# Squares summed on VectorE at seven stage fronts, twelve more low parts by accumulating DMA, and half of the second panel ahead of the first mean, in a two-block transformer kernel

## The chip, the core and the metric

The kernel runs on one core of one Trainium2 chip. The metric is the device time of one launch in microseconds (us). The engines are named as the profile names them: PE (TensorE, matrix products), PEld (its weight loads), DVE (VectorE), ACT (ScalarE), POOL (GpSimd) and SP (SyncE, which issues the DMAs of raw weights). Each engine works through its own instructions in the order in which they were written into its queue; an instruction whose operands are not there holds up all that is queued behind it on that engine.

## What is computed

Two blocks over a sequence of 512 rows with model width 1024, all in fp32. Cut to what matters:

```python
# first block, layer 0 (causal conformer convolution) and layer 1 (forgetting attention)
hn = rmsnorm(h, mix_norm[i])
h = h + conformer_conv(hn, ...)          # layer 0: hn @ w_pw1, a * sigmoid(g), 31 taps, layernorm, silu, @ w_pw2
h = h + fox_attention(hn, ...)           # layer 1: 16 heads, softmax with cumulated forget gates, @ w_o
hn = rmsnorm(h, ffn_norm[i])
h = h + square(relu(hn @ ffn_w1[i])) @ ffn_w2[i]
h = h + sigmoid(rmsnorm(h, ple_norm[i]) @ ple_w_gate[i]) * (p[i] @ ple_w_proj[i])
...
x = rmsnorm(h, final_norm)               # end of the first block
# second block
h = rms_norm(x, mix_norm_gain)           # -> w_in: recurrent, block-sparse and memory branches, gates, w_out
x = x + merged @ w_out
h = rms_norm(x, ffn_norm_gain)
x = x + (gelu(dwconv(h @ w_gate)) * (h @ w_up)) @ w_down
return rms_norm(x, final_norm_gain)
```

The rows matter here for one thing: every stage begins with a root mean square over the 1024 columns of h, which needs the squares of all eight column groups of h summed and averaged before the stage's results can be scaled.

## The kernel before, in words

**Layout.** The 512 rows lie along the free dimension, the 1024 columns in eight tiles of 128 partitions (f = 0 to 7), so h is eight tiles of 128x512. Products run on PE at fp32 accuracy as three products of reduced-precision halves: `mm3` issues hi times xh, hi times xl, lo times xh, where a weight is hi + lo and an activation xh + xl.

**Weights.** They come as panels of 128x2048 fp32 (1 MB), in the order of `_KEYS`, through SP's queue into two raw buffers (`load`). `splitting` cuts a panel in four pieces of 128x512; `part` casts a piece to hi on ACT and subtracts to get lo, on DVE, or on POOL for the families in `LO_POOL` (`pw1`, `vm`, `o`). For the panels in `SEVEN`, `lows_by_dma` makes three of the four lo pieces another way: ACT writes minus raw into lo, rounded as hi is, and a DMA on POOL's queue adds the raw weight from memory to it, which leaves raw minus hi with no work for DVE (`accumulate`). hi and lo have two buffers each, so a panel's piece can be written when PE has read that of the panel two before it. `prefetch` loads and starts to split the next panel while the current one is used; the delay `PREFETCH` holds the splitting back.

**Fronts.** `Front` takes the h tiles of a new stage as they are finished: `split_into` makes xh (ACT) and xl (DVE), `square` makes the square of the tile (ACT), and `Norm.add` adds it to a running sum. The first tile's square is the sum's start; the six adds after it run on POOL and the last on DVE. The very first front has two sums (`two=True`): two adds on POOL, five on DVE. When the last square is in, `chain` computes the mean on PE (eight small products, tiles `tp<-C,sq`), adds epsilon on DVE (`s<-tp`), takes the power on POOL (`s<-s,mhalf`), and spreads it over the partitions on PE (`tp<-C,s`) and ACT (`rbc`). The products with xh and xl run ahead of it, since the scale is applied to their results: in the order of PE's queue the mean stands among them.

**Order.** A recording-time model (`Flow`, with a cost for each engine) decides in which order the parallel strands are written into the engines' queues. Nothing is decided on the chip. A change of costs or of engines therefore shifts the order of much that isn't named in the diff.

**Stages that matter below.** The convolution's first products, `pw1` (eight panels; each gives a gate half and a value half of one f); the mixed front of the attention layer (`mix1`); the second feed-forward front `w1(1,0,0)`, whose panel is used in blocks (`BLOCKED`) so that its first products need all four pieces; the gates `plg(l,0..3)`; the panels `xa(0)`, `xa(1)` on which the second block begins, beside the last norm of the first block.

Of the kernel before, what the change touches and what calls it, by code (L numbers as in the profile page):

```python
# [11 lines left out]
AF = mybir.ActivationFunctionType  # L12
# [3 lines left out]
S = 512  # L16
# [211 lines left out]
def kernel(ctx: ExitStack, tc, gain0, x_t, p_t, mem_t, vec, w, w_f, w_lru, rows, consts, out):  # L228
# [64 lines left out]
    def col(name, f, tap=0, per=8):  # L293
        c = _VOFF[name] + tap * per + f
        return V[:, c:c + 1]
# [3 lines left out]

    def load(i, pieces=1):  # L300
        if i < len(_KEYS) and i not in raws:
            if _KEYS[i] in SEVEN:
                early[i] = flow.spawn(lows_by_dma(i), 0.0, 2)
            r = wp.tile([128, PW], F32, name=nm("raw"), tag="raw", bufs=2)
            raws[i] = r
            c = PW // pieces
            return [lambda k=k: dma(r[:, c * k:c * k + c], w[i, :, c * k:c * k + c]) for k in range(pieces)]
        return []

    class Panel:  # L310


        def __init__(self, key):
            self.key, self.blocked = key, key[0] in BLOCKED
            self.q = {}
# [6 lines left out]
        def cols(self, a, m):  # L322

            return tuple(self.piece(n, a // S)[:, a % S:a % S + m] for n in ("hi", "lo"))

        def weights(self, k, c0, width, m):

            if self.blocked:
                return self.cols(S * (c0 // 128 * (3 - k % 2) + (1 - c0 // 128) * (k % 2)) + k // 2 * 128, m)
            return self.cols(k * width + c0, m)  # L330

    class Plain:
        def __init__(self, hi, lo):
            self.hi, self.lo = hi, lo

        def weights(self, k, c0, width, m):
            a = k * width + c0
            return self.hi[:, a:a + m], self.lo[:, a:a + m]

    def part(i, k, pieces, low):  # L340

        if i not in parts:
            parts[i] = Panel(_KEYS[i])
        c = PW // pieces
        r = raws[i][:, c * k:c * k + c]
        hi, lo = parts[i].cols(c * k, c)
        gain = GAINED.get(_KEYS[i][0])
        if gain is not None:
            g = col(gain, k)
            act.activation(hi, r, AF.Copy, scale=g)  # L350
            dve.scalar_tensor_tensor(lo, r, g, hi.bitcast(F32), op0=ALU.mult, op1=ALU.subtract)
        else:
            act.copy(hi, r)
            low.tensor_sub(lo, r, hi.bitcast(F32))
# [12 lines left out]
    def lows_by_dma(i):  # L367

        r = raws[i]
        for b in range(3):  # L370
            c = slice(S * b, S * b + S)
            yield lambda: cur[0] >= i - 1 or (i - 2, b) in spent
            yield r[:, c]
            yield flow.quiet(act, patience=HOLD)
            if i not in parts:
                parts[i] = Panel(_KEYS[i])
            lo = parts[i].piece("lo", b)
            act.mul(lo, r[:, c], -1.0)
            yield lo
            accumulate(lo, w[i, :, c])  # L380
# [148 lines left out]
    def splitting(i):  # L529
        if _KEYS[i] in SEVEN:  # L530
            yield from sums_split(i)
            return
        pieces = KT if _KEYS[i][0] in GAINED else 4
        low = pool if _KEYS[i][0] in LO_POOL else dve
        c = PW // pieces
        for k in range(pieces):
            yield raws[i][:, c * k:c * k + c]
            yield flow.quiet(act, low, patience=HOLD)
            part(i, k, pieces, low)

    ahead = {}
# [9 lines left out]
    def prefetch(i, delay):  # L551
        for g in load(i) + load(i + 1):
            g()
        if i < len(_KEYS) and _KEYS[i] not in FULL32:
            ahead[i] = flow.spawn(splitting(i), 0.2 if _KEYS[i] in SEVEN else delay, 2)

    def panel(key, fetch=True):
        i = _PIDX[key]
        cur[0] = max(cur[0], i)
        if i not in ahead:  # L560
            ahead[i] = flow.spawn(splitting(i), 0.0, 2)
        flow.finish(ahead[i])
        if i in early:
            flow.finish(early[i])
        if fetch:
            prefetch(i + 1, PREFETCH)
        return parts[i]

    def mm3(ps, wh, wl, xh, xl, start, stop):
# [4 lines left out]
    def gemm(ps, pan, c0, xs, width=256, ks=None, m=128):  # L574

        if isinstance(pan, tuple):
            pan = Plain(*pan)
        n = len(xs)
        for k in range(n) if ks is None else ks:
            if xs[k] is None:  # L580
                flow.until(lambda: xs[k] is not None)
            wh, wl = pan.weights(k, c0, width, m)
            mm3(ps, wh, wl, xs[k][0], xs[k][1], k == 0, k == n - 1)

# [48 lines left out]
    class Norm:  # L633


        def __init__(self, n=S, total=KT, two=False):
            self.n, self.left, self.two = n, total, two
            self.parts = []

        def add(self, t, g=None):  # L640
            n = self.n
            self.left -= 1
            q = slot(p="sq")
            act.activation(q[:, :n], t, AF.Square, scale=1.0 if g is None else g)
            if len(self.parts) <= self.two:
                self.parts.append(q)
                return
            s = self.parts[self.left % (1 + self.two)]
            (dve if self.left % 2 and self.two or self.left == 0 else pool).tensor_add(s[:, :n], s[:, :n], q[:, :n])
            if self.left == 0 and self.two:  # L650
                dve.tensor_add(s[:, :n], s[:, :n], self.parts[1][:, :n])
            self.sum = s
# [31 lines left out]
    class Front:  # L684


        def __init__(self, g=None, two=False):
            self.g = g
            self.xs = [None] * KT
            self.norm = Norm(two=two)  # L690
            self.r4 = self.rbc = self.side = None

        def add(self, f, t):
# [134 lines left out]
    def conv_pool(fs):  # L828
        for f in fs:
            yield lambda: us[f] is not None  # L830
            u = us[f]
            yield u
            a = slot(p="acc")
            act.activation(a, u, AF.Identity, scale=col("w_dw", f, TAPS - 1), bias=col("b_dw", f))
            for j in range(TAPS - 1):
                sh = TAPS - 1 - j
                t = slot(p="tap")
                act.activation(t[:, sh:], u[:, :S - sh], AF.Copy, scale=col("w_dw", f, j))
                pool.tensor_add(a[:, sh:], a[:, sh:], t[:, sh:])
                yield flow.quiet(pool, slack=POOL_AHEAD)  # L840
            acc[f] = a
            ended.append(f)
# [20 lines left out]
    for f in range(KT):  # L863
# [5 lines left out]
        if f == 2:  # L869
# [4 lines left out]
            for q in range(KT // 2):  # L874
                t = slot(p="mt")
                for k in range(2):
                    dma(t[:, MEM * k:MEM * k + MEM], mem_t[2 * q + k])
                    mt.append(t[:, MEM * k:MEM * k + MEM])
        pa, pg = bank(), bank()
        if f == 0:  # L880
            couter(pan, front.xs, banks=[pa, pg])
        else:
            gemm(pg, pan, 128, front.xs)
        rbc = front.get()
        ta, tg = slot(), slot()
# [1014 lines left out]
MEM_PERIOD = 9.0  # L1900
LO_POOL = ("pw1", "vm", "o")
HOLD_SUMS = 0.3
BLOCKED = ("w1", "gu")
SEVEN = {("w1", l, c, i) for l in range(2) for c in range(1, 4) for i in range(4)}
SEVEN |= {("gu", m) for m in range(8, 24)}
# [156 lines left out]
```

## Time and profile before

| what | us |
|---|---|
| median of three runs (2130.28 to 2131.87) | 2131.7 |
| the profiled execution | 2132.37 |
| its span, first to last instruction | 2129.5 |
| PE busy | 2078.7 (98%) |
| DVE busy | 1428.5 (67%) |
| ACT busy | 1159.2 (54%) |
| POOL busy | 473.2 (22%) |
| mean granted TensorE clock | 0.992 |

The span is the stretch that the trace covers; 2.9 us of the profiled time lie outside it. Times in the trace are counted from the first instruction. PE's busy time counts each matmul until its modelled end; matmuls of 128x512 follow one another every 0.227 us at the full clock and every 0.427 us at half of it, and where PE waits, a row carries the idle time and the instruction that ended it in square brackets. Nearly all instructions carry line L83, the line of the helper that records them, so groups are told apart by tile names.

### The profile page before, as it was taken

What the parts mean: (1) busy time and instruction counts of PE and PEld (TensorE: products, weight loads), DVE (VectorE), ACT (ScalarE), POOL (GpSimd) and SP (SyncE); (2) the same over time, 40 slices, a digit from 0 to 9 for tenths busy, and PEclk for the clock granted to TensorE, in tenths of its full rate; (3) what the DMA queues carried; (4) which work ended last, traced back from release to release, by engine and by line L of the source; (5) the groups of instructions that cost most, each with busy time, mean ns of one, the idle gap of its engine ahead of it and who ended that gap; (6) DMA issues with size and microseconds to landing.
All of it is one profiled execution on the core that took longest, in us unless ns stands there. A gap on an engine that the chain in (4) does not pass through costs nothing.

```text
span 2129.5 us, 30406 instructions
## 1 busy us (share of the span) xinstructions
PE 2078.7 (98%) x11360; PEld 1783.7 (84%) x11360; DVE 1428.5 (67%) x2534; ACT 1159.2 (54%) x2372; POOL 473.2 (22%) x500
## 2 busy tenths in 40 slices
PE   7999999999999999899999999999999999999998
PEld 6867889899878887789898887878888888899997
DVE  5997557566576887666565677775574557776683
ACT  5776446456445676455464553665462333485672
POOL 4882101101121326401011121331010010020212
PEclk9999999999999999999999999999999999999999
DMA  5215236547322111236455523112222423375661
GB/s 185 99 61 197 88 115 155 129 129 183 115 81 86 61 62 61 70 106 142 125 153 127 170 87 123 62 61 101 99 71 88 139 80 119 112 158 147 148 170 60
DMA packets 58050, 240.73 MB, mean 113 GB/s; under 512 B 6824, under 2 KB 10152, under 8 KB 35504
## 3 DMA queue, kind: packets, MB, share of 16 engines
q1 hardware_dynamic: 40048, 206.81, 28.7%
q0 software_dynamic: 17280, 31.46, 9.1%
q8 instruction: 89, 1.46, 0.3%
q10 hardware_dynamic: 576, 0.52, 0.1%
q14 instruction: 57, 0.47, 0.1%
HBM read 229.00 MB, written 9.77 MB: 112 GB/s over the span
## 4 chain that ended last, share of the span: by engine, by line
PE 78%; DVE 10%; ACT 7%; issue 2%; POOL 2%; DMA 1%; SPq 0%; DVEq 0%; ACTq 0%; POOLq 0%
PE mm L83 69%; PE sc L83 6%; DVE t L83 2%; DVE sc L83 2%; ACT hi L83 2%; PE tp L83 1%; ACT t L83 1%; DVE lo L83 1%; PE ptp L83 1%; DVE xl L83 1%; POOL acc L83 1%; DVE h L83 1%; ACT lo L83 1%; DVE xc L83 1%; ACT sh L83 1%
## 5 line engine op out<-in xcount | busy, mean ns | idle before, releaser
L83 PE MATMUL mm<-xh,hi 128*128 128x512 f32 (+1 forms) x2096 | 797.6, 381 | 8.7 <-ACT hi L83 7.3
L83 PE MATMUL mm<-xh,lo 128*128 128x512 f32 (+1 forms) x2096 | 796.1, 380 | 7.0 <-DVE lo L83 6.6
L83 PE MATMUL mm<-xl,hi 128*128 128x512 f32 (+1 forms) x2096 | 795.4, 379 | 0.0
L83 PEld LDWEIGHTS mm<-xh,hi 128*128 128x128 f32 x2096 | 397.1, 189 | 79.6 <-ACT hi L83 7.6
L83 PEld LDWEIGHTS mm<-xh,lo 128*128 128x128 f32 x2096 | 396.8, 189 | 79.4 <-DVE lo L83 9.1
L83 PEld LDWEIGHTS mm<-xl,hi 128*128 128x128 f32 x2096 | 396.9, 189 | 69.5
L83 ACT CAST hi<-raw 128x512 fp32r<-128x512 f32 x596 | 347.2, 617 | 111.9 <-PE mm L83 96.3
L83 DVE TENSOR_TENSOR lo<-raw,hi 128x512 fp32r<-128x512 f32 x424 | 291.3, 724 | 60.5 <-ACT hi L83 58.6
L362 POOL DMA_DIRECT2D lo<-in_w x120 | 104.0, 866 | 760.5 <-ACT lo L83 699.5
L83 DVE TENSOR_TENSOR h<-mm,h 128x512 f32<-128x512 f32 (+1 forms) x113 | 75.5, 670 | 242.4 <-PE mm L83 242.3
L83 POOL TENSOR_TENSOR sq<-sq,sq 128x512 f32<-128x512 f32 (+1 forms) x69 | 84.5, 1226 | 437.2 <-ACT sq L83 436.6
L83 ACT ACTIVATE lo<-raw 128x512 fp32r<-128x512 f32 x120 | 76.5, 637 | 81.5 <-PE mm L83 81.5
L83 POOL TENSOR_SCALAR P<-P,s 128x128 f32<-128x128 f32 (+2 forms) x112 | 64.2, 578 | 243.4 <-DVE s L83 195.7
L83 DVE TENSOR_TENSOR sl<-sum,sh 128x512 fp32r<-128x512 f32 x120 | 82.4, 686 | 15.6 <-ACT sh L83 14.9
L83 PE MATMUL mm<-ch,sh 128*128 128x256 f32 x320 | 90.6, 283 | 0.0
L83 PE MATMUL mm<-cl,sh 128*128 128x256 f32 x320 | 90.6, 283 | 0.0
L83 PE MATMUL mm<-ch,sl 128*128 128x256 f32 x320 | 90.6, 283 | 0.0
L83 ACT ACTIVATE xh<-h,V 128x512 fp32r<-128x512 f32 x40 | 28.6, 722 | 112.9 <-DVE h L83 112.9
L83 PE MATMUL mm<-ch,hi 128*128 128x256 f32 x352 | 88.0, 285 | 1.6 <-ACT p L83 1.6
L83 ACT CAST sh<-sum 128x512 fp32r<-128x512 f32 x120 | 75.4, 628 | 20.1 <-DVE sum L83 20.1
L83 PE MATMUL mm<-ch,lo 128*128 128x256 f32 x288 | 81.5, 283 | 0.0
L83 POOL TENSOR_TENSOR acc<-acc,tap 128x482 f32<-128x482 f32 (+29 forms) x60 | 77.2, 1286 | 13.1 <-ACT tap L83 9.5
(295 smaller groups left out, 3908.1 us busy)
## 6 DMA issues: line engine op xcount, KB each, us to landing
raw<-in_w SPq DMA_DIRECT2D x175, 1024.0 KB
lo<-in_w POOLq DMA_DIRECT2D x120, 256.0 KB, 5.2
prd<-pr SPq DMA_DIRECT2D x16, 256.0 KB
pr<-prd SPq DMA_DIRECT2D x16, 256.0 KB
h<-in_x_t SPq DMA_DIRECT2D x8, 256.0 KB
resid<-h SPq DMA_DIRECT2D x8, 256.0 KB
h<-resid SPq DMA_DIRECT2D x8, 256.0 KB
out<-out SPq DMA_DIRECT2D x12, 128.0 KB
```

What stands on the lines that cost most here:

```text
L83: f(out, *args, **kw)
L362: nc.gpsimd.dma_start(out, src, accum_op=ALU.add)
```

## The change

1. `Norm` has a new flag `alone`; every `Front` but the first has it set, and then all seven adds of the squares run on DVE. Fronts changed: both feed-forward and both gate stages of the first block, the attention's mix, the second block's mix and feed-forward. The first block's final norm, the memory's norm and the last norm keep their adds on POOL.
2. `LO_DMA`: twelve panels (`w1(1,0,0)`, `w1(1,0,1)`, `xa(0)`, `xa(1)` and the eight `plg`) get all four lo pieces by ACT and accumulating DMA.
3. The gate half of panel `pw1(1)` is written ahead of the first front's `get()`, so ahead of its mean (`second`, `whole=False`, `ready`).
4. `LO_DVE`: the lo pieces of `pw1(1)` and `pw1(2)` are made on DVE in place of POOL.
5. The prefetch of the first panels has no delay. Since `panel(("pw1", 1))` is now called twice, `prefetch(2)` runs twice, and panel `pw1(2)` is split twice.

```diff
@@ load @@
-            if _KEYS[i] in SEVEN:
+            if _KEYS[i] in SEVEN or _KEYS[i] in LO_DMA:
                 early[i] = flow.spawn(lows_by_dma(i), 0.0, 2)
@@ part @@
+        if _KEYS[i] in LO_DMA:
+            act.copy(parts[i].piece("hi", k), raws[i][:, c * k:c * k + c])
+            return
@@ lows_by_dma @@
-        for b in range(3):
+        for b in range(3 if _KEYS[i] in SEVEN else 4):
@@ splitting @@
-        low = pool if _KEYS[i][0] in LO_POOL else dve
+        low = pool if _KEYS[i][0] in LO_POOL and i not in LO_DVE else dve
...
-            yield flow.quiet(act, low, patience=HOLD)
+            yield flow.quiet(*((act,) if _KEYS[i] in LO_DMA else (act, low)), patience=HOLD)
@@ panel @@
-        flow.finish(ahead[i])
+        if whole:
+            flow.finish(ahead[i])
...
-            prefetch(i + 1, PREFETCH)
+            prefetch(i + 1, PREFETCH if i > 1 else 0.0)
+        if not whole:
+            flow.until(lambda: i in parts)
@@ Norm.add @@
-            (dve if self.left % 2 and self.two or self.left == 0 else pool).tensor_add(s[:, :n], s[:, :n], q[:, :n])
+            (dve if self.alone or self.left % 2 and self.two or self.left == 0 else pool).tensor_add(
+                s[:, :n], s[:, :n], q[:, :n])
@@ Front @@
-            self.norm = Norm(two=two)
+            self.norm = Norm(two=two, alone=not two)
@@ the pw1 loop @@
         if f == 0:
             couter(pan, front.xs, banks=[pa, pg])
-        else:
+            second = bank(), bank()
+            gemm(second[1], panel(("pw1", 1), whole=False), 128, front.xs)
+        elif f > 1:
             gemm(pg, pan, 128, front.xs)
@@ constants @@
+LO_DVE = (1, 2)
+LO_DMA = {("w1", 1, 0, 0), ("w1", 1, 0, 1), ("xa", 0), ("xa", 1)} | {("plg", l, i) for l in range(2) for i in range(4)}
```

**PE at the start, before.** `mm_161` and `mm_162` are the first panel's results, `tp_244` the mean, `tp_261` its spreading, `mm_278` the gate half of `pw1(1)`; `x4` counts equal rows.

```order
L83 MATMUL mm_162<-xl_150,hi_153 128x512
L83 MATMUL mm_162<-xh_149,lo_154 128x512
L83 MATMUL tp_244<-C,sq_191 128x1 x4
L83 MATMUL tp_261<-C,s_250 128x128 x4
L83 MATMUL mm_278<-xh_109,hi_236 128x512
L83 MATMUL mm_278<-xl_110,hi_236 128x512
L83 MATMUL mm_278<-xh_109,lo_237 128x512
```

The same place after; the gate half is now `mm_237`.

```order
L83 MATMUL mm_162<-xh_149,lo_154 128x512
L83 MATMUL mm_237<-xh_109,hi_240 128x512
L83 MATMUL mm_237<-xl_110,hi_240 128x512
L83 MATMUL mm_237<-xh_109,lo_241 128x512
L83 MATMUL tp_247<-C,sq_191 128x1 x4
L83 MATMUL mm_237<-xh_113,hi_240 128x512
L83 MATMUL mm_237<-xl_114,hi_240 128x512
L83 MATMUL mm_237<-xh_113,lo_241 128x512
L83 MATMUL mm_237<-xh_121,hi_256 128x512
L83 MATMUL mm_237<-xl_122,hi_256 128x512
L83 MATMUL mm_237<-xh_121,lo_257 128x512
L83 MATMUL mm_237<-xh_125,hi_256 128x512
```

Three products stand ahead of the mean, and seven more between it and its spreading.

**DVE at the start, after**: the end of the first front's sum (`sq_191`), then the lo pieces of the second panel, which stood on POOL.

```order
L83 TENSOR_TENSOR sq_191<-sq_191,sq_227 128x512
L83 TENSOR_TENSOR sq_191<-sq_191,sq_195 128x512
L83 CAST identb<-C 128x128
L83 CAST maskb<-C 128x128
L83 TENSOR_TENSOR lo_241<-raw_157,hi_240 128x512
L83 TENSOR_SCALAR s_252<-tp_247 128x4
L83 TENSOR_TENSOR lo_257<-raw_157,hi_256 128x512
```

The third of PE's moved products reads `lo_241`, which DVE makes behind the sum.

**DVE at the front of the second feed-forward stage, before.** `h_8402` to `h_8416` are the eight h tiles, `lo_9049`, `9061`, `9081`, `9095` the four low pieces of `w1(1,0,0)`, `sq_9019` the sum of squares.

```order
L83 SCALAR_TENSOR_TENSOR xl_9016<-h_8406,V,xh_9015 128x512
L83 TENSOR_TENSOR lo_9049<-raw_8872,hi_9048 128x512
L83 TENSOR_TENSOR lo_9061<-raw_8872,hi_9060 128x512
L83 SCALAR_TENSOR_TENSOR xl_9028<-h_8408,V,xh_9027 128x512
L83 SCALAR_TENSOR_TENSOR xl_9035<-h_8410,V,xh_9034 128x512
L83 TENSOR_TENSOR h_8414<-mm_9043,h_8414 128x512
L83 TENSOR_TENSOR lo_9081<-raw_8872,hi_9080 128x512
L83 SCALAR_TENSOR_TENSOR xl_9047<-h_8412,V,xh_9046 128x512
L83 TENSOR_TENSOR lo_9095<-raw_8872,hi_9094 128x512
L83 TENSOR_TENSOR h_8416<-mm_9076,h_8416 128x512
```

The same stretch of DVE's queue after (h tiles `8426` to `8440`, sum `sq_9055`).

```order
L83 SCALAR_TENSOR_TENSOR xl_9052<-h_8430,V,xh_9051 128x512
L83 SCALAR_TENSOR_TENSOR xl_9064<-h_8432,V,xh_9063 128x512
L83 TENSOR_TENSOR sq_9055<-sq_9055,sq_9101 128x512
L83 SCALAR_TENSOR_TENSOR xl_9071<-h_8434,V,xh_9070 128x512
L83 TENSOR_TENSOR h_8438<-mm_9079,h_8438 128x512
L83 TENSOR_TENSOR sq_9055<-sq_9055,sq_9120 128x512
L83 SCALAR_TENSOR_TENSOR xl_9083<-h_8436,V,xh_9082 128x512
L83 TENSOR_TENSOR sq_9055<-sq_9055,sq_9129 128x512
L83 TENSOR_TENSOR h_8440<-mm_9107,h_8440 128x512
```

The lo pieces are gone from DVE, and the adds of squares stand in their place. On POOL the six adds are gone, and its queue at this place reads, after (the lo pieces of `w1(1,0,0)`, then of `w1(1,0,1)`, and the mean's power `s_9205`):

```order
L371 DMA lo_9013<-in_w 128x512
L371 DMA lo_9152<-in_w 128x512
L371 DMA lo_9165<-in_w 128x512
L371 DMA lo_9175<-in_w 128x512
L83 TENSOR_TENSOR s_9205<-s_9204,mhalf 128x4
L371 DMA lo_9191<-in_w 128x512
```

The power now stands behind seven DMAs that each wait for ACT's negated copy.

**ACT where the second block begins, after**: `lo_12962` to `lo_12981` are the negated copies for `xa(1)`, `t_12950` the last gate's sigmoid, `sq_13001` the last square of the first block's final norm.

```order
L83 ACTIVATE lo_12974<-raw_12850 128x512
L83 ACTIVATE t_12950<-t_12950 128x512
L83 ACTIVATE lo_12981<-raw_12850 128x512
L83 CAST hi_12991<-raw_12850 128x512
L83 CAST hi_12993<-raw_12850 128x512
L83 CAST hi_12997<-raw_12850 128x512
L83 ACTIVATE sq_13001<-h_8440,V 128x512
```

Before, the corresponding square (`sq_12933`) had one cast between it and the square of the tile before.

## Rows read from the trace of the kernel before

**Rows 1.** The page: busy time per engine, then groups (count, busy us, mean ns).
```profile
PE 2078.7 (98%) x11360; PEld 1783.7 (84%) x11360; DVE 1428.5 (67%) x2534; ACT 1159.2 (54%) x2372; POOL 473.2 (22%) x500
...
L83 DVE TENSOR_TENSOR lo<-raw,hi 128x512 fp32r<-128x512 f32 x424 | 291.3, 724 | 60.5 <-ACT hi L83 58.6
L362 POOL DMA_DIRECT2D lo<-in_w x120 | 104.0, 866 | 760.5 <-ACT lo L83 699.5
...
L83 ACT ACTIVATE lo<-raw 128x512 fp32r<-128x512 f32 x120 | 76.5, 637 | 81.5 <-PE mm L83 81.5
```

**Rows 2.** What PE waited for: us in total, times, longest.
```profile
PE tp L83 <- DVE sq L83: 13.3, 6, 4.2
```

**Rows 3.** PE at the start: start, us, tile, idle before and what ended it.
```profile
20.08 0.39 PE L83 MATMUL mm<-xh,lo 128*128 128x512 f32 x1
24.67 1.86 PE L83 MATMUL tp<-C,sq 128*128 128x1 f32 x8 [4.21 <-DVE sq L83]
27.89 2.08 PE L83 MATMUL tp<-C,s 128*128 128x128 f32 x8 [1.35 <-POOL s L83]
...
42.72 0.39 PE L83 MATMUL mm<-xh,hi 128*128 128x512 f32 x1
```

**Rows 4.** DVE and POOL at the start, the same columns.
```profile
18.21 6.40 DVE L83 TENSOR_TENSOR sq<-sq,sq 128x512 f32<-128x512 f32 x4 [0.35 <-ACT sq L83]
...
20.69 3.38 POOL L83 TENSOR_TENSOR lo<-raw,hi 128x512 fp32r<-128x512 f32 x2
```

**Rows 5.** Windows: stretch, its us, busy (instructions) per engine, granted clock, DMA share, GB/s.
```profile
24.30:34.30 10.00, 8.27 (x28) 7.18 (x29) 2.79 (x7) 3.95 (x6) 4.57 (x4) 0.51 0.28 96
827.90:832.00 4.10, 1.44 (x8) 0.90 (x8) 4.10 (x5) 0.30 (x2) 3.60 (x4) 1.00 0.00 0
...
1338.00:1342.00 4.00, 4.00 (x11) 3.23 (x12) 3.59 (x5) 1.65 (x3) 1.06 (x1) 0.58 0.00 0
...
120.00:150.00 30.00, 30.00 (x97) 17.88 (x96) 30.00 (x48) 23.63 (x48) 26.84 (x22) 1.00 0.14 54
```

**Rows 6.** All engines around the second feed-forward front, 869 to 900 us.
```profile
878.56 0.72 ACT L83 ACTIVATE xh<-h,V 128x512 fp32r<-128x512 f32 x1 [8.59 <-DVE h L83]
...
877.83 2.05 DVE L83 TENSOR_TENSOR h<-mm,h 128x512 f32<-128x512 f32 x3 [7.14 <-PE mm L83]
...
884.00 0.73 DVE L83 SCALAR_TENSOR_TENSOR xl<-h,V,xh 128x512 fp32r<-128x512 f32 x1
...
886.25 0.39 PE L83 MATMUL mm<-yh,lo 128*128 128x512 f32 x1
...
887.17 6.61 POOL L83 TENSOR_TENSOR sq<-sq,sq 128x512 f32<-128x512 f32 x4
887.56 1.75 DVE L83 SCALAR_TENSOR_TENSOR xl<-h,V,xh 128x512 fp32r<-128x512 f32 x1
...
894.38 0.80 PE L83 MATMUL mm<-xh,lo 128*128 128x512 f32 x1 [6.62 <-DVE lo L83]
...
897.11 0.63 PE L83 MATMUL mm<-xh,lo 128*128 128x512 f32 x1
```

**Rows 7.** Landing times of the accumulating DMAs (tile lo, POOL).
```profile
DMA to landing us min/median/max: 3.9/5.2/8.9
```

**Rows 8.** PE at the attention's front and where the second block begins.
```profile
635.60 1.02 PE L83 MATMUL tp<-C,sq 128*128 128x1 f32 x8 [1.89 <-DVE sq L83]
...
1290.73 1.84 PE L83 MATMUL tp<-C,sq 128*128 128x1 f32 x8 [4.03 <-DVE sq L83]
...
1296.41 0.63 PE L83 MATMUL mm<-xh,hi 128*128 128x512 f32 x1
```

**Rows 9.** DVE and ACT ahead of that second wait.
```profile
1283.80 0.69 DVE L83 TENSOR_TENSOR t<-mm,rbc 128x512 f32<-128x512 f32 x1
...
1289.89 0.69 DVE L83 TENSOR_TENSOR sq<-sq,sq 128x512 f32<-128x512 f32 x1 [0.26 <-ACT sq L83]
...
1285.16 0.61 ACT L83 ACTIVATE t<-t 128x512 f32<-128x512 f32 x1
```

More of the change, by code (lines that the diff above doesn't have):

```diff
@@ L324, in cols, with ready @@
             return tuple(self.piece(n, a // S)[:, a % S:a % S + m] for n in ("hi", "lo"))
+        def ready(self, k, c0, width):
+            return self.blocked or ("lo", (k * width + c0) // S) in self.q
         def weights(self, k, c0, width, m):
@@ L334, in __init__, with ready @@
             self.hi, self.lo = hi, lo
+        def ready(self, k, c0, width):
+            return True
         def weights(self, k, c0, width, m):
@@ L555, in prefetch, with panel @@
             ahead[i] = flow.spawn(splitting(i), 0.2 if _KEYS[i] in SEVEN else delay, 2)
-    def panel(key, fetch=True):
+    def panel(key, fetch=True, whole=True):
         i = _PIDX[key]
@@ L581, in gemm @@
                 flow.until(lambda: xs[k] is not None)
+            flow.until(lambda: k < len(xs) and pan.ready(k, c0, width))
             wh, wl = pan.weights(k, c0, width, m)
@@ L633, with __init__ @@
     class Norm:
-        def __init__(self, n=S, total=KT, two=False):
-            self.n, self.left, self.two = n, total, two
+        def __init__(self, n=S, total=KT, two=False, alone=False):
+            self.n, self.left, self.two, self.alone = n, total, two, alone
             self.parts = []
@@ L833, in conv_pool @@
             a = slot(p="acc")
-            act.activation(a, u, AF.Identity, scale=col("w_dw", f, TAPS - 1), bias=col("b_dw", f))
-            for j in range(TAPS - 1):
+            n = PE_TAPS.get(f, 0)
+            if n:
+                yield lambda: f in pre
+                yield pre[f]
+                act.activation(a, pre[f], AF.Identity, bias=col("b_dw", f))
+            else:
+                act.activation(a, u, AF.Identity, scale=col("w_dw", f, TAPS - 1), bias=col("b_dw", f))
+            for j in range(TAPS - max(n, 1)):
                 sh = TAPS - 1 - j
@@ L878 @@
                     mt.append(t[:, MEM * k:MEM * k + MEM])
-        pa, pg = bank(), bank()
+        if f == 1:
+            pa, pg = second
+        else:
+            pa, pg = bank(), bank()
         if f == 0:
             couter(pan, front.xs, banks=[pa, pg])
-        else:
+            second = bank(), bank()
+            gemm(second[1], panel(("pw1", 1), whole=False), 128, front.xs)
+        elif f > 1:
             gemm(pg, pan, 128, front.xs)
```

## The prediction, made before the changed kernel was run

> **What bounds the kernel now.** The busy times come first: PE is busy for 98% of the span, DVE for 67%, ACT 54%, POOL 22% [rows 1]. A change that takes no work from PE can only win where PE waits, so the next view is the list of PE's waits [rows 2]. The means of squares cost 13.3 us in six waits, the longest 4.2. A wait has a second price, to be read in the windows by clock: in the 10 us behind the first front's wait the granted clock is 0.51 [rows 5], that is the lower level of 1.2 GHz, and matmuls follow each other at about twice their distance.
>
> Four waits matter here.
>
> The start. PE's last matmul of the first panel begins at 20.08, the mean only at 24.67, after 4.21 us idle; then come 1.35 us for POOL's power, and the second panel's first matmuls only behind that [rows 3]. The cause is the sum on DVE: four adds take 6.40 us, with two POOL subtractions beside them [rows 4].
>
> The second feed-forward front. PE stands 6.62 us for a lo piece and then runs seven matmuls at the lower clock, to 897.11 [rows 6]. DVE is not idle in that time, it is slow: an xl that begins beside a POOL add takes 1.75 us, one that begins without it 0.73 [rows 6]. So an operation with two SBUF inputs that starts beside a POOL add waits out that add. The Trainium skill says the same in "SBUF — State Buffer", "Who interferes with whom": DVE with two SBUF inputs and a GpSimd instruction that reads SBUF exclude one another, and the later one blocks until the first is done; by that rule each POOL add can cost DVE a whole operation, and these rows agree.
>
> The attention's front: 1.89 us. The beginning of the second block: 4.03 us, then ten matmuls at half clock [rows 8].
>
> **The change part by part.** The sum is made against the profiled run of 2132.4 us (2129.5 span and 2.9 outside); the median of the runs lies 0.7 below it.
>
> *Squares on DVE, lo pieces of twelve panels off DVE.* Forty-two adds come to DVE (seven fronts, six each, about 0.69 us [rows 9]: 29 us) and 48 lo subtractions go (0.724 each: 35 us). DVE's load so hardly changes; what goes is POOL's exclusion. ACT gets 48 negations at 0.637 (31 us), POOL 48 DMA issues at 0.866 (42 us) in place of some 42 adds [rows 1].
>
> Second feed-forward front. By the order, DVE's queue from the first h tile of this front to the end of the sum holds 23 operations. In the trace it reaches that place at 877.83 [rows 6]; at some 0.65 us each, with no POOL add beside them, the sum ends at about 893. PE's last matmul of the stage before is at 886.25 [rows 6], 30 of the new stage's products stand ahead of the mean, 30 x 0.227 = 6.8, so PE asks for it at 893.1. That comes out even; I allow a wait of 0.5. The lo pieces now come by DMA: the negations stand right behind the last yh on ACT, ahead of the first xh, in 8.59 us in which ACT was idle [rows 6], so at some 870 to 873.5; the DMAs land by 3.9 to 8.9 us later [rows 7], so by 882.5, and are needed from 886.9 on. Gain: 6.6 idle + 0.4 for the restart + 1.5 for seven matmuls at half clock (0.2 each), less 0.5: 8.0. For the next panel `w1(1,0,1)` the issues come at about 890 to 895, and the landings, by 5.2 us 895 to 900, by 8.9 us 899 to 904, stand against a need at 899 to 905: margins between 4 and 0 us. The power of the mean is queued behind three of these issues on POOL; each is 0.87 and waits for ACT, and the third is through about when the sum is.
>
> Attention's front: no POOL add beside DVE's last operations (about 0.9 saved), and the mean stands eight products (1.8) later in PE's order: of 1.89 + 0.39 all goes. Gain 2.0, between 1 and 2.3.
>
> Beginning of the second block. The first block's last norm keeps its adds on POOL, but fewer POOL adds stand beside DVE. Last gate result at 1283.8 [rows 9]. Before, the chain from there took 6.8 us to the sum's end (1290.6). After: 0.7 product, 0.6 sigmoid (1285.16), then ACT has a negation and three casts ahead of the square that it did not have in this place (to 3.6 after the gate result); square 0.7, add 0.7: 4.9. PE arrives at 2.9 after it in the trace, by the order four matmuls later, 3.7. A wait of 1.2 stays of 4.03. The halved clock, seen behind waits of 4.0 or more, then does not come, as it does not behind the wait of 2.67 at 828 [rows 5]. Gain 2.8 + 0.9 (the mean's eight small products took 1.84, at the attention's front 1.02) + ten matmuls by 0.2: 5.7; a second mean close behind may cost some of it. I take 5.0, between 2 and 6.
>
> Gate panels. PE has no wait at these in the trace. The negation of a piece waits until PE has read the piece two panels before, and all else on ACT waits behind it in order, sigmoids among it; the order puts it where the recording model thinks it free. From the 120 existing ones: ACT stood 81.5 us in front of them in all, 0.68 each [rows 1], with no wait on PE shown for their lo. The smallest margin that I work out for landing at 8.9 us is 3 us. Cost 0, bounded by 0 and 12 panels x 1 us.
>
> *Half the second panel ahead of the first mean.* By the order only three products go ahead, and the third needs a lo piece that DVE makes behind the sum. The sum ends earlier: the last two of the four adds lose POOL's subtractions beside them, about 1 us each, so at 22.6 instead of 24.6. Then two casts (0.3) and the lo piece (0.7): 23.6. PE stands still from 20.8 to 23.6, 2.8 us instead of 4.2. Then the mean (1.0) and seven products (1.6) instead of a wait for the power; the next lo piece stands behind `s<-tp` in DVE's queue, which costs about 0.5. The second panel's 48 matmuls then end at 36.5 instead of 42.9 if the clock holds, and at about 41 if it falls. Waits of 4.0, 4.2 and 6.6 were followed by the low level, one of 2.67 was not [rows 5]; against that, a stretch at 1338 to 1342, behind two short waits among small products, shows 0.58 [rows 5]. I take the row that 2.8 is nearest to: the clock holds, gain 6.4. Of this something is given back: from 60 to 170 us DVE is the loaded engine (30.00 of 30.00 us in one window, PE beside it 30.00 [rows 5]), and it starts its convolution as much earlier as the second panel's results come, some 5.5. The doubled splitting adds four casts on ACT and four subtractions on DVE (2.9 us by rows 1), in a stretch where DVE was 2.79 of 10 us busy. I take 1.4 given back, bounds 0 and 5: gain 5.0.
>
> *Prefetch delay, `pw1` on DVE.* Contained above; POOL loses eight subtractions.
>
> Sum: 8.0 + 2.0 + 5.0 + 5.0 = 20.0. 2132.4 - 20.0 = 2112.4; against the median 2111.7. I say **2112**.
>
> **The rivals.** (a) *The clock falls at the start all the same.* 2.8 us idle lie between 2.67 (held) and 4.03 (fell). Then the start gives about 1, and the waits left at the second block may also bring the low level (2.9 less): 2112 + 4 to 7, so 2116 to 2119. For it: the start has two short waits close together, as the stretch at 1338 that fell. [...]
>
> (b) *Only the front at 887 is mended.* DVE's order is right but the chains through ACT set the means: the second block's wait stays at 3, and convolution and layernorm give back all of the start. Then 8 + 2 + 1 = 11: 2121. For it: DVE fully loaded from 60 to 170.
>
> (c) *Slower: the negations block ACT.* A negation whose piece PE has not yet read holds every xh, square, sigmoid and cast behind it. With eleven of the twelve panels at places where ACT is on the way of the results, each with a blocked time of over 3 us (the margin worked out above), PE would wait the excess; landings at the upper end of rows 7 would add to it. 12 panels by 2 us are 24 and eat up the 20 gained: from that point on, 2 us per panel, the change costs. 3 us per panel give 2132 - 20 + 36 = 2148. Against it: 120 such negations in the trace cost ACT 0.68 each, and PE none. The Trainium skill ("SBUF — State Buffer", the box on "DVE blocks DMA") says that DVE copies and casts in its two-port mode keep GpSimd from writing descriptors; by it the landings would grow where such operations run. The spread of 3.9 to 8.9 may hold that, but nothing in the trace shows more.
>
> (d) *Part 3 does nothing*, since the third product waits for the same sum as the mean: the start gains only the two DVE adds (2) and 1.3 for the power: 2114 to 2115. This lies within the forecast's range.
>
> **How the numbers follow.** Forecast with (d): 0.55, range 2106 to 2117. (a): 0.17, about 2117. (b): 0.15, 2121, of which 0.04 reach 2127 to 2136, no change. (c): 0.08, of which 0.06 above 2136 and 0.02 between. A better end, with all remaining waits of the touched fronts gone (some 4 more), 0.05: 2104. A measurement of this kernel can tell 0.2% from no change, about 4.3 us: so faster means below 2127.4, slower above 2136.0. Faster 0.88, same 0.06, slower 0.06. The range leaves out the better end and most of (c) and the worst of (b): 2104 to 2125.
>
> **What would show it.** Right: no PE wait over 1 us at 880 to 900; no DVE operation over 1.3 us there; wait at the attention's mean under 0.5; at the second block about 1.2, clock near 1.0; at the start PE idle 2.8 us before the third product, the second panel finished at 36.5; mean clock above 0.995. Wrong: PE waiting for a lo piece whose DMA landed late, an ACT row `lo<-raw` with a long idle time ahead and a sigmoid or xh behind it for which PE waits, or PE waiting in 170 to 210 for the convolution's end by more than 2 us.

## The result, and the profile after

The changed kernel takes 2114.89 us in the median of six runs (2112.78 to 2117.95), the kernel before beside it 2130.92. The ratio is 0.9926, 95% interval 0.9916 to 0.9936, so about 15.8 us or 0.74% faster. The forecast was 2112 (2104 to 2125), faster by more than 0.2% with a chance of 0.88. The profiled execution took 2117.41 us, 2.5 more than the median, and its span is 2115.6, which is 13.9 less than before's.

Part 1 of the page after, and then what PE waited for (us in total, times, longest); these answer to [rows 1] and [rows 2].

```profile
PE 2075.4 (98%) x11360; PEld 1781.7 (84%) x11360; DVE 1408.7 (67%) x2540; ACT 1188.6 (56%) x2424; POOL 444.9 (21%) x498
...
PE mm L83 <- ACT hi L83: 8.4, 2, 7.3
PE tp L83 <- DVE sq L83: 3.7, 4, 1.6
PE mm L83 <- DVE lo L83: 2.9, 2, 1.9
PE mm L83 <- DVE xl L83: 2.9, 1, 2.9
```

The means cost 3.7 us where they cost 13.3, and the 6.6 us for a lo piece are gone. The 7.3 us for a hi piece stood in the trace before too. New is the last line: one wait of 2.9 us for an xl.

PE issues 11360 matmuls in both kernels, in nearly the same order. Where the n-th matmul begins (n counted from 0), after minus before, therefore tells where time went:

| n-th matmul | place | before, us | after, us | difference |
|---|---|---|---|---|
| 80 | in the second panel | 35.46 | 28.96 | -6.5 |
| 580 | convolution stage, memory products | 157.77 | 152.36 | -5.4 |
| 700 | behind the layer norm's mean | 186.57 | 182.24 | -4.3 |
| 760 | convolution's output product | 200.85 | 201.92 | +1.1 |
| 3000 | ahead of the attention's front | 598.19 | 598.97 | +0.8 |
| 3190 | behind it | 641.69 | 640.34 | -1.35 |
| 4400 | end of the attention | 845.44 | 845.41 | 0.0 |
| 4700 | behind the second feed-forward front | 914.04 | 906.98 | -7.1 |
| 6900 | in the second block | 1307.39 | 1293.74 | -13.6 |

Three fronts gained about what was expected. The start won 6.5 us in this pair of traces and lost all of it, with one more, by the output product of the convolution. The attention lost 1.35.

**The second feed-forward front** (compare [rows 6]): PE at its first products, then DVE from the first h tile on.

```profile
886.87 0.39 PE L83 MATMUL mm<-xh,lo 128*128 128x512 f32 x1
888.38 0.50 PE L83 MATMUL mm<-xh,hi 128*128 128x512 f32 x1 [1.12 <-ACT hi L83]
...
877.77 2.05 DVE L83 TENSOR_TENSOR h<-mm,h 128x512 f32<-128x512 f32 x3 [7.15 <-PE mm L83]
881.14 0.75 DVE L83 SCALAR_TENSOR_TENSOR xl<-h,V,xh 128x512 fp32r<-128x512 f32 x1 [1.32 <-ACT xh L83]
...
892.40 0.74 DVE L83 SCALAR_TENSOR_TENSOR xl<-h,V,xh 128x512 fp32r<-128x512 f32 x1
893.25 0.69 DVE L83 TENSOR_TENSOR sq<-sq,sq 128x512 f32<-128x512 f32 x1
```

No xl takes more than 0.75 us, the sum ends at 893.94, and PE's one wait is 1.12 us for a hi piece that ACT made late. The 1.32 us in front of the first xl are ACT's: the fourth negation for a lo piece waited 6.17 us for PE, and the first xh stood behind it.

```profile
879.86 0.63 ACT L83 ACTIVATE lo<-raw 128x512 fp32r<-128x512 f32 x1 [6.17 <-PE sc L83]
```

From there ACT works without a gap until it has made the late hi piece, so this negation may have cost PE the 1.12 us too; no run parts that.

**The convolution's output product**: PE, then DVE in the same stretch of the changed kernel.

```profile
192.41 0.49 PE L83 MATMUL mm<-xh,hi 128*128 128x512 f32 x1 [0.33 <-ACT pr L83]
195.77 0.80 PE L83 MATMUL mm<-xl,hi 128*128 128x512 f32 x1 [2.87 <-DVE xl L83]
...
200.63 0.63 PE L83 MATMUL mm<-xh,hi 128*128 128x512 f32 x1
...
182.77 3.68 DVE L83 TENSOR_TENSOR acc<-acc,tp 128x512 f32<-128x512 f32 x6 [1.52 <-PE tp L83]
187.23 0.69 DVE L83 TENSOR_TENSOR lo<-raw,hi 128x512 fp32r<-128x512 f32 x1 [0.78 <-ACT hi L83]
190.16 0.69 DVE L83 TENSOR_TENSOR lo<-raw,hi 128x512 fp32r<-128x512 f32 x1 [2.24 <-ACT hi L83]
192.91 0.69 DVE L83 TENSOR_TENSOR lo<-raw,hi 128x512 fp32r<-128x512 f32 x1 [2.06 <-ACT hi L83]
194.43 0.69 DVE L83 TENSOR_TENSOR lo<-raw,hi 128x512 fp32r<-128x512 f32 x1 [0.83 <-ACT hi L83]
195.03 3.70 DVE L83 TENSOR_TENSOR xl<-acc,xh 128x512 fp32r<-128x512 f32 x6
```

DVE is idle for 5.1 us between 187.9 and 194.4, and PE waits for an xl from it from 192.9 on: four lo pieces, each waiting for ACT, stand ahead of the xl in its queue. Behind the wait PE runs at half clock until 201.

### The profile page after: what moved, and what is told of

It reads as the page before. It is cut to its first block, busy times and chain, and to the rows that moved or that the text cites. A ratio compares the mean times of both kernels' runs of the same rounds, so it can differ in the third digit from the quotient of the medians.

```text
span 2115.6 us, 30453 instructions
## 1 busy us (share of the span) xinstructions
PE 2075.4 (98%) x11360; PEld 1781.7 (84%) x11360; DVE 1408.7 (67%) x2540; ACT 1188.6 (56%) x2424; POOL 444.9 (21%) x498
## 4 chain that ended last, share of the span: by engine, by line
PE 80%; DVE 8%; ACT 8%; issue 2%; POOL 0%; DVEq 0%; ACTq 0%; POOLq 0%
PE mm L83 72%; PE sc L83 6%; ACT hi L83 2%; ACT t L83 2%; PE ptp L83 1%; PE tp L83 1%; DVE t L83 1%; ACT lo L83 1%; DVE mm L83 1%; DVE xc L83 1%; DVE sc L83 1%; ACT sh L83 1%; ACT xh L83 1%; DVE lo L83 1%; DVE xl L83 1%
## 5 line engine op out<-in xcount | busy, mean ns | idle before, releaser
L371 POOL DMA_DIRECT2D lo<-in_w x168 | 147.0, 906 | 912.0 <-ACT lo L83 845.1
L83 DVE TENSOR_TENSOR lo<-raw,hi 128x512 fp32r<-128x512 f32 x388 | 255.0, 696 | 52.5 <-ACT hi L83 50.2
L83 ACT ACTIVATE lo<-raw 128x512 fp32r<-128x512 f32 x168 | 105.4, 633 | 103.6 <-PE mm L83 95.6
L83 DVE SCALAR_TENSOR_TENSOR sc<-u,V,sc 128x511 f32<-128x511 f32 (+23 forms) x116 | 77.8, 732 | 0.4
L83 ACT ACTIVATE z<-z 128x512 f32<-128x512 f32 x64 | 40.4, 631 | 63.2 <-DVE z L83 63.1
```

Of the source, the lines that this page charges most:

```text
L83: f(out, *args, **kw)
L371: nc.gpsimd.dma_start(out, src, accum_op=ALU.add)
```

## The experiments

All ratios are to the kernel before, run beside; 1% is 21.3 us. "Squares" names the engine that adds the squares at the seven fronts, "third panel split" whether panel `pw1(2)` is split once or twice.

| kernel | squares | low pieces by DMA | start | third panel split | ratio | 95% interval |
|---|---|---|---|---|---|---|
| changed kernel | DVE | 12 panels | new | twice | 0.9926 | 0.9916 to 0.9936 |
| sq_only | DVE | none | old | once | 0.9921 | 0.9908 to 0.9935 |
| lows_only | POOL | 12 | old | once | 0.9960 | 0.9947 to 0.9972 |
| no_start | DVE | 12 | old | once | 0.9918 | 0.9905 to 0.9932 |
| start_only | POOL | none | new | twice | 1.0017 | 1.0008 to 1.0026 |
| start_once | POOL | none | new | once | 0.9987 | 0.9978 to 0.9996 |
| no_double | DVE | 12 | new | once | 0.9894 | 0.9880 to 0.9908 |
| sq_start_once | DVE | none | new | once | 0.9915 | 0.9901 to 0.9929 |
| no_plg | DVE | 4 | new | twice | 0.9918 | 0.9904 to 0.9932 |
| ffn1_pool | one front on POOL | 12 | new | twice | 0.9935 | 0.9922 to 0.9948 |
| pw2_pool | DVE | 12 | new | twice | 0.9918 | 0.9904 to 0.9932 |
| charged | DVE | 12 | new | once, order of twice | 0.9919 | 0.9905 to 0.9932 |
| all_alone | DVE, all norms | none | new | once | 0.9962 | 0.9948 to 0.9975 |

### One part at a time

`sq_only`, the kernel before with the squares alone:

```diff
-            self.norm = Norm(two=two)
+            self.norm = Norm(two=two, alone=not two)
```

> The kernel before with one part of the change alone: the squares of the seven fronts are added on VectorE. Theory A (a POOL add beside a DVE operation with two SBUF inputs costs DVE about 1 us, and taking the adds off POOL is worth it although DVE gets 42 more operations): the attention's front gains its 2 us, the second feed-forward front 3 to 6 of its 8.5, the second block's beginning 2 to 4 of its 7: 2120 to 2124. Rival B (what counts is DVE's load: 42 more adds and no lo piece less): no gain, 2129 to 2135.

Measured: 2113.84 against 2130.82, 17 us faster, beyond what theory A gave and against rival B: one flag brings as much as the whole change. DVE at the second feed-forward front of this kernel, with all its lo pieces still on it, and PE's wait there:

```profile
878.02 0.75 DVE L83 SCALAR_TENSOR_TENSOR xl<-h,V,xh 128x512 fp32r<-128x512 f32 x1
...
881.76 0.68 DVE L83 TENSOR_TENSOR lo<-raw,hi 128x512 fp32r<-128x512 f32 x1
...
882.49 0.50 PE L83 MATMUL mm<-xh,lo 128*128 128x512 f32 x1 [2.09 <-DVE lo L83]
```

With six more operations than before, DVE is done sooner: nothing there takes over 0.75 us, and PE waits 2.09 us instead of 6.62, at full clock. The order of DVE's queue doesn't explain it: 18 operations stand ahead of the fourth lo piece where 16 stood, and yet it is done 12.0 us after the first h tile begins instead of 16.5. This is the direct evidence that the POOL adds beside DVE, and neither DVE's own load nor its order, made this front late.

`lows_only`, the kernel before with the twelve panels in `LO_DMA`, squares on POOL.

> The kernel before with one part alone: the low pieces of the twelve panels by ACT and accumulating DMA, the squares still added on POOL. Theory A (exclusion): DVE loses 48 subtractions, but every xl beside a POOL add still takes about 1.75 us; the second feed-forward front gains 4 to 6, the second block's beginning 1 to 3, the attention's front nothing: 2122 to 2126. Rival B (load): nearly all of the 15 us that the whole change gained behind the start: 2115 to 2118.

Measured: 2122.14, 8.7 us faster, in theory A's range. PE's waits in it: the means still cost 11.5 us, and a lo piece by DMA came late once.

```profile
PE tp L83 <- DVE sq L83: 11.5, 7, 3.8
...
PE mm L83 <- DMA lo<-in_w: 2.0, 1, 2.0
...
902.59 0.50 PE L83 MATMUL mm<-xh,lo 128*128 128x512 f32 x1 [1.95 <-DMA lo<-in_w]
```

`no_start`, the changed kernel with the start as before:

```diff
-LO_DVE = (1, 2)
+LO_DVE = ()
...
-            prefetch(i + 1, PREFETCH if i > 1 else 0.0)
+            prefetch(i + 1, PREFETCH)
...
-            second = bank(), bank()
-            gemm(second[1], panel(("pw1", 1), whole=False), 128, front.xs)
-        elif f > 1:
+        else:
             gemm(pg, pan, 128, front.xs)
```

> The changed kernel with the start as before: no half panel ahead of the first mean, low pieces of the second and third panels on POOL, the prefetch delay back. Theory A (what the start gains is given back at the convolution's output product, where PE waits 2.87 us for an xl and then runs at half clock): 2112 to 2116, no slower than the changed kernel. Rival B (the start is worth the 5 us that were forecast): 2118 to 2121.

Measured: 2113.83, no slower than the changed kernel. Rival B is out: as written, the new start brings nothing. Squares and low pieces together (0.9918) are no better than the squares alone (0.9921): apart from the start, the two cover nearly the same waits. In the traces the low pieces add 0.9 us at the second feed-forward front (matmuls 4400 to 4700) and 1.4 at the second block's beginning (4700 to 6900), less than these ratios can tell from nothing.

`start_only`, the start alone, with the third panel split twice.

> The kernel before with only the start changed: half the second panel ahead of the first mean, low pieces of the second and third panels on VectorE, no prefetch delay there, the third panel split twice. Theory A (given back at the convolution's output product): 2129 to 2133, and in the trace a wait for xl of 2 to 3.5 us at about 195 us. Rival B: 2125 to 2127, no such wait.

Measured: 2134.67 against 2130.82, ratio 1.0017 (1.0008 to 1.0026): slower, more than theory A allowed. In its trace PE waits 2.86 us for an xl at 194.8, as in the changed kernel.

### The gates and one front

`no_plg` leaves the eight gate panels' lo pieces on DVE.

> The changed kernel with the eight gate panels' low pieces on VectorE as before; only four panels are left to the DMA. Theory A (PE never waited at the gates, and the second block's beginning gains by the squares and the xa panels): 2113 to 2117, unchanged. Rival B (the gate panels' 32 subtractions are what makes the second block's beginning late): 2118 to 2121, and a wait of 2 us or more at its mean.

Measured: 2115.47, unchanged; theory A. So 32 of the 48 DMAs make no difference to the time.

`ffn1_pool` puts one front's squares back on POOL:

```diff
     nf = Front(lambda f: col("ffn1", f))
+    nf.norm.alone = False
```

> The changed kernel with the squares of the second feed-forward front alone back on POOL; its low pieces still come by DMA. Theory A (exclusion): six operations of DVE at 878 to 895 take 1.3 to 1.8 us, and PE waits 2 to 5 us more at this front: 2117 to 2121. Rival B (DVE has six adds less to do, so it is done sooner): 2113 to 2115.

Measured: 2118.19, 3.3 us slower in the medians and 1.9 by the ratios, whose intervals overlap widely. In the traces this front gives back 3.5 of the 7.1 us that it had gained. POOL, DVE and PE in its trace, and a window as in [rows 5]:

```profile
885.55 7.75 POOL L83 TENSOR_TENSOR sq<-sq,sq 128x512 f32<-128x512 f32 x5 [2.02 <-ACT sq L83]
...
885.92 1.44 DVE L83 SCALAR_TENSOR_TENSOR xl<-h,V,xh 128x512 fp32r<-128x512 f32 x1
...
889.27 1.51 DVE L83 SCALAR_TENSOR_TENSOR xl<-h,V,xh 128x512 fp32r<-128x512 f32 x1 [0.19 <-ACT xh L83]
893.33 0.69 DVE L83 TENSOR_TENSOR sq<-sq,sq 128x512 f32<-128x512 f32 x1 [2.56 <-POOL sq L83]
...
894.08 1.05 PE L83 MATMUL tp<-C,sq 128*128 128x1 f32 x8 [1.11 <-DVE sq L83]
...
894.00:899.00 5.00, 4.92 (x24) 4.52 (x25) 0.19 (x2) 0.46 (x2) 3.81 (x5) 0.73 0.78 168
```

Theory A has the time, but not the way to it: two xl, not six operations, take over 1.3 us, and PE waits 1.11 us more, not 2 to 5; the rest of the 3.5 us comes behind the wait, mostly from the clock, 0.73 in the window where the changed kernel has 1.00. What PE waits for here is the sum, which waits 2.56 us for POOL: the adds in a row on POOL are late in themselves. With the lo pieces off DVE no wait of PE on a slowed xl is left.

### What ate the start's gain

`pw2_pool` takes the four lo pieces ahead of the xl off DVE:

```diff
-LO_POOL = ("pw1", "vm", "o")
+LO_POOL = ("pw1", "vm", "o", "pw2")
```

> The changed kernel with the low pieces of the convolution's four output panels on POOL in place of VectorE. In the changed kernel DVE's queue has four of these pieces, each waiting for ACT's hi, ahead of all eight xl for which PE waits at 195 us. Theory A (the order of DVE's queue makes the wait): the wait of 2.87 us and the half clock behind it go, 2108 to 2112. Rival B (the xl are late because the layer norm's chain through ACT is late): the wait stays, 2113 to 2117.

Measured: 2114.81, no difference clear of the error (0.9918 against 0.9926). The wait for xl and the half clock behind it are gone, as theory A has it (granted clock 1.00 from 190 to 202), and two shorter waits stand in their place, PE in the trace of this kernel:

```profile
193.50 0.50 PE L83 MATMUL mm<-xh,hi 128*128 128x512 f32 x1 [1.04 <-ACT pr L83]
195.72 0.50 PE L83 MATMUL mm<-xh,hi 128*128 128x512 f32 x1 [1.26 <-ACT pr L83]
```

So DVE's order was the last link only: theory A has the mechanism, rival B the time.

`no_double` splits the third panel once:

```diff
-        if i < len(_KEYS) and _KEYS[i] not in FULL32:
+        if i < len(_KEYS) and _KEYS[i] not in FULL32 and i not in ahead:
```

> The changed kernel without the second splitting of the third panel: four casts on ACT and four subtractions on VectorE less at 28 to 42 us. The wait of 0.98 us at 40.5 for a low piece should go. Theory A (the wait at the convolution's output product swallows what is gained before it): 2113 to 2117, unchanged. Rival B (the early microsecond counts): 2112 to 2114.

Measured: 2109.33, 5.6 us faster than the changed kernel and the fastest of all; against theory A, and more than rival B gave for one early microsecond. PE around the layer norm's mean, first in `no_double`, then in the changed kernel:

```profile
174.82 1.02 PE L83 MATMUL tp<-C,sq 128*128 128x1 f32 x8 [0.35 <-DVE sq L83]
175.70 1.97 PE L83 MATMUL mm<-raw,mt 128*128 128x256 f32 x8
177.51 1.05 PE L83 MATMUL tp<-C,s 128*128 128x128 f32 x8
178.40 1.46 PE L83 MATMUL mm<-raw,mt 128*128 128x256 f32 x6
```

```profile
178.83 1.02 PE L83 MATMUL tp<-C,sq 128*128 128x1 f32 x8 [0.83 <-DVE sq L83]
...
181.58 1.16 PE L83 MATMUL tp<-C,s 128*128 128x128 f32 x8
```

In `no_double`, as in the kernel before (x8 and x6 there too), fourteen of the memory's products stand behind the mean and give PE 3.4 us of work while DVE and ACT finish the layer norm. In the changed kernel they stand ahead of the mean, and PE comes to the output product that much too early. The xl are in time in `no_double`, one behind each lo piece in DVE's queue, and PE doesn't wait for them:

```profile
187.40 0.69 DVE L83 TENSOR_TENSOR lo<-raw,hi 128x512 fp32r<-128x512 f32 x1 [3.63 <-ACT hi L83]
188.00 0.68 DVE L83 TENSOR_TENSOR xl<-acc,xh 128x512 fp32r<-128x512 f32 x1
...
191.83 0.50 PE L83 MATMUL mm<-xh,hi 128*128 128x512 f32 x1 [0.39 <-ACT pr L83]
192.17 0.40 PE L83 MATMUL mm<-xl,hi 128*128 128x512 f32 x1
```

`charged` parts the order from the work. It issues the second splitting no more, but charges its cost to the recording model:

```diff
+    def charged(i):
...
+        for k in range(4):
+            yield raws[i][:, c * k:c * k + c]
+            yield flow.quiet(act, low, patience=HOLD)
...
+            flow.account(act, [hi], [rr], act.cost("copy", hi, [rr]))
+            flow.account(low, [lo], [rr, hi], low.cost("tensor_sub", lo, [rr, hi]))
```

Its queues are those of the changed kernel, row for row, without the eight instructions.

> The changed kernel without the eight instructions of the third panel's second splitting, but with their cost still charged to the recording model, so that every other instruction stands in the same order as in the changed kernel. It parts work from order. Theory A (the second splitting costs by the order that it makes the model write, with four low pieces ahead of all xl on VectorE near 190 us): 2113 to 2117, with a wait for an xl of 2 us or more before the convolution's output product. Rival B (the eight instructions themselves cost the 5.6 us): 2108 to 2111, no such wait.

Measured: 2113.71, theory A. DVE of this kernel at the place:

```profile
190.87 0.69 DVE L83 TENSOR_TENSOR lo<-raw,hi 128x512 fp32r<-128x512 f32 x1 [0.83 <-ACT hi L83]
191.47 3.69 DVE L83 TENSOR_TENSOR xl<-acc,xh 128x512 fp32r<-128x512 f32 x6
```

The work of the second splitting is worth 0.0007 of the ratio (0.9926 to 0.9919), within the error; in the trace it is a wait of 0.98 us for a lo piece at 41.9, with its restart 1.3 us. The order that it makes the model write is worth 0.0025 (0.9919 to 0.9894), some 5 us, with intervals that just touch. In the traces `charged` falls 2.9 us behind `no_double` by the output product; another 1.3 come in the attention, where the queues of the two are the same and the clock fell in `charged` alone.

`start_once` is the kernel before with the start changed and the panel split once.

> The kernel before with only the start changed, and the third panel split once. Theory A (the start by itself is worth the forecast 5 us once the second splitting is gone): 2124 to 2128. Rival B (the start's lead is given back in the convolution stage, where VectorE is full, whatever the splitting): 2130 to 2134.

Measured: 2127.07 against 2129.98, 0.9987 (0.9978 to 0.9996), 2.8 us: theory A, with the smaller part of its 5. Beside squares and low pieces it is worth more, 0.9918 to 0.9894 from `no_start` to `no_double`, about 5 us, with intervals that just touch. The second splitting turns this gain into the loss of `start_only`.

`sq_start_once` leaves the low pieces by DMA out of `no_double`.

> The changed kernel without the twelve panels' low pieces by DMA and with the third panel split once: squares and start alone. Theory A (the low pieces by DMA add nothing once the squares are off POOL): 2108 to 2111, as the kernel with both at 2109.3. Rival B (they do part of the work at the fronts): 2112 to 2116, with a wait for a low piece of over 2 us at the second feed-forward front that brings the half clock.

Measured: 0.9915 (0.9901 to 0.9929) against 0.9894 with them. Between the two theories: the ratios speak for 4.5 us, the medians for 2.8, and the intervals overlap. In the trace PE waits 2.09 us for a lo piece at the second feed-forward front, at full clock. Beside `no_double`'s, this trace loses the same 0.9 us at that front and 1.4 at the second block's beginning as `sq_only` beside `no_start`. So the low pieces by DMA are worth some 2 us beside the squares in two pairs of traces; the ratios don't show it clear of their error.

`all_alone` goes on from there and puts the remaining norms' adds on DVE too.

> The same as squares and start alone with the third panel split once, and also the adds of the first block's final norm, of the memory's norm and of the last norm on VectorE. Theory A (wherever a POOL add stands beside VectorE it costs): 1 to 3 us faster than the same without, 2106 to 2109, the two waits at the last norm 0.5 to 1 us shorter. Rival B (in the convolution stage VectorE is full, and six more adds there push the layer norm back): 2110 to 2113.

Measured: 2120.05 against 2129.98, 0.9962, about 10 us slower than without. PE ahead of the output product in its trace:

```profile
195.34 0.51 PE L83 MATMUL mm<-xh,hi 128*128 128x512 f32 x1 [1.08 <-ACT pr L83]
199.23 0.80 PE L83 MATMUL mm<-xl,hi 128*128 128x512 f32 x1 [3.38 <-DVE xl L83]
```

The wait for an xl is back, longer than in the changed kernel. Rival B in sign, far beyond it in size, and again with the four lo pieces ahead of the xl in DVE's queue and no memory product behind the layer norm's mean in PE's. Of the 12.1 us between the two traces 10.7 arise by the output product. Whether the six adds themselves or the order cost it wasn't parted here.

## Why the prediction was right, and where it was not

**The fronts.** Second feed-forward front: forecast 8.0, read off the matmuls 7.1; the sum was to end at 893 and ended at 893.94, the allowed wait of 0.5 was 1.12 plus a restart, over the 1 us that the forecast named as its sign. Attention's front: 2.0 forecast, 2.1 found. Second block's beginning: 5.0 forecast, 6.5 found, since the wait there is 0.6 and not 1.2, and the halved clock stayed away as said. Sum of the three: 15.0 forecast, 15.7 found. But the credit was shared wrongly. The forecast gave the gain to squares and low pieces together; `sq_only` has 13.4 of the 15.7 (6.1, 2.2 and 5.2) without a single new DMA.

**The exclusion** of POOL adds and two-input DVE operations is confirmed where it was read, an xl of 0.75 us with no POOL add beside and of 1.44 and 1.51 with one. `ffn1_pool` adds what the forecast left out: moved off POOL, the sum is also finished sooner in itself.

**The low pieces by DMA.** Landing times were 3.9 to 11.4 us (median 5.4), longer at the end than the 8.9 assumed, and no matmul waited for one in the changed kernel. Rival (c) didn't come in size, but both its parts were seen: `lows_only` waited 1.95 us for a DMA, and at the second feed-forward front the fourth negation was not done by 873.5, as forecast, but began at 879.86, with the first xh behind it.

**The start is the step that failed.** It was to bring 5.0 us and brought none: `no_start` is no slower than the changed kernel, and the fronts alone account for the 15.8 us measured. The time came within the range because the range was wide enough for that. Its mechanism was right as far as it went: with POOL's subtractions off it the sum's four adds take 4.41 us instead of 6.40, about the 2 us forecast, and PE idles 1.93 us instead of 4.21. That the second panel's last matmul begins at 36.21, forecast 36.5, is luck: ACT's first squares begin 1.3 us earlier than in the trace before, which isn't the change's doing (the other kernels with the old start have it too), so the idle time is shorter than the 2.8 us forecast; against that the clock, which was to hold, fell. DVE and PE there, against [rows 3, 4]:

```profile
16.91 4.41 DVE L83 TENSOR_TENSOR sq<-sq,sq 128x512 f32<-128x512 f32 x4 [0.35 <-ACT sq L83]
...
22.25 0.50 PE L83 MATMUL mm<-xh,lo 128*128 128x512 f32 x1 [1.93 <-DVE lo L83]
```

The term "1.4 given back, bounds 0 and 5" was wrong: 7.6 went by the output product, beyond its upper bound, and the forecast's own sign of being wrong, a wait of over 2 us for the convolution's end, came with 2.87. It was priced as work on a loaded DVE, and the second splitting was put down at 2.9 us of free time. The work shows as 1.3 us; what costs most is neither that nor DVE's load: the eight instructions shift the recording model's clock, the model writes fourteen covering products ahead of the layer norm's mean and four lo pieces ahead of the xl, and PE runs out of work 150 us later. In `no_double`, without this order, 1.6 us is given back between the same matmuls, which is what the forecast put. How much more the order costs in one execution depends on the clock: `charged`, with the same order and the same wait of 2.87 us, gives back 4.4. The order of the changed kernel shows both moves before any run; the forecast weighed only DVE's load in that stage.

**The clock.** The forecast let the clock hold behind 2.8 us of idle time, since it held behind 2.67 at 828. The same place in the changed kernel, windows (stretch, us, busy per engine, granted clock, DMA share, GB/s):

```profile
829.90:833.30 3.40, 3.40 (x13) 3.12 (x14) 2.79 (x7) 2.11 (x5) 0.88 (x2) 0.56 0.00 0
...
24.30:27.80 3.50, 3.50 (x14) 3.00 (x13) 1.83 (x4) 0.03 (x1) 0.91 (x1) 0.57 0.33 82
195.00:202.00 7.00, 6.23 (x16) 4.91 (x17) 6.75 (x13) 4.96 (x10) 0.00 (x0) 0.54 0.72 247
```

Here the wait is 2.54 us and the clock fell, to the lower of its levels; that accounts for the 1.35 us that the attention lost: in `sq_only`, whose clock did not fall there, the difference to before is -7.2 us at matmul 3200 and still -7.4 at 4400. At the start it fell behind 1.93. So rival (a) came true in part, and a row from one execution didn't bear the decision that was laid on it.

## What to carry to other kernels

An add on POOL was not free where DVE worked beside it: one flag that moved 42 adds to the engine with more to do gained 17 us, as much as all parts together. Where a model decides the order while the program is written, the cost of an edit includes what it does to the order far behind it; compare the queues at the next places where an engine waits, and if in doubt charge the model without issuing the work, which parts the two in one run. Try the parts one by one: here one part carried the change, one mostly repeated it, and one lost by a slip (a panel split twice), without which the kernel is the fastest of all at 2109.33.

## What was not expected of the hardware

Waits of much the same length are followed by either clock: behind 2.67 us at 828 the granted clock was 1.00, behind 2.54 us at the same products 0.56, behind 1.93 us at the start 0.57 and behind 2.87 us in the changed kernel 0.54. Two kernels whose queues are the same in the attention show it best, first `no_double` behind a wait of 2.52 us, then `charged` behind 2.53:

```profile
822.80:826.30 3.50, 3.47 (x19) 3.05 (x20) 3.44 (x8) 2.97 (x8) 0.98 (x2) 1.00 0.00 0
...
825.30:828.70 3.40, 3.40 (x13) 3.12 (x14) 2.81 (x7) 2.08 (x5) 0.88 (x2) 0.58 0.00 0
```

Behind 1.89 us at the attention's front it was 1.00 in the kernel before and 0.56 in `start_once`. What decides between the two wasn't found. Whoever prices a wait of 2 to 3 us needs both outcomes. And the start of one execution varies with no change to it: the second panel's last matmul begins at 42.72 in the kernel before and at 37.99, 40.53 and 40.44 in the three other kernels with the old start. In the trace of the kernel before the last tiles of x came about 1 us later than in the others, and the granted clock from 25 to 35 us was 0.55, against 1.00, 0.66 and 0.71. So 2 to 5 of the 6.5 us that the first trace showed there were that one execution's.
